# TensorE's order through attention, one norm chain for q and k, and a 16-byte offset in a hybrid decoder layer

## The chip, the cores and the metric

The kernel runs on one core of one Trainium2 chip. The metric is the device time of one execution in microseconds; three executions before the change took 2040.69, 2043.23 and 2045.04 us, a median of 2043.23 us. All work is in fp32; TensorE (PE) multiplies, ScalarE (ACT) and VectorE (DVE) split weights and do the element-wise work, GpSimd (POOL) helps with a few products and issues small DMAs, and SyncE (SP) issues the weight loads.

## The reference

One decoder layer on 256 tokens of width 2048. An SSD (Mamba-2) branch and an attention branch run from the same normed input, are merged by sigmoid gates, and a causal ConvFFN follows. What matters here is the attention branch (one block of 256 keys, so it is plain causal attention with a relative bias):

```python
q = rmsnorm(q, q_norm_w) * (D ** -0.5)          # 16 heads, D = 128
k = rmsnorm(k, k_norm_w)
s_own = jnp.einsum('bhqd,bhkd->bhqk', qi, kown)
s_own = jnp.where(dist >= 0, s_own + bias_own, -jnp.inf)
p = jax.nn.softmax(logits, axis=-1)
out = jnp.einsum('bhqk,bhkd->bhqd', p_own, vown)
...
y_attn = moba_attention(q, k, v, ...) @ w_attn_out[l]
x = x + (g_ssm * y_ssm + g_attn * y_attn) @ w_out[l]
```

## The kernel before

**Units.** Every weight matrix is streamed once, in units of 128 x 2048 floats (1 MB). For each unit SP loads `wraw`; for each of its two halves ACT writes a rounded high part `whi` (line 181) and DVE the rest, the low part `wlo` (line 182), both in the matmul's fp32r type, three buffers each. `cm_chunk` (lines 211 to 219) then multiplies a half: for each of 8 blocks of 128 columns the high part meets the high and the low part of the activations (lines 215 and 216), and 8 matmuls with the low part follow (line 218). A unit is 48 matmuls of 128x128 weights and 256 moving columns. `tm_chunk` (lines 371 to 383) does the same for the values v with 512 moving columns, 24 matmuls for a unit.

**Stages.** Three of four parts of v; eight head pairs (`attn_pair(j)`, four units each: q, q, k, k), with the last part of v between pairs 5 and 6; six units of the attention gate; sixteen units of `wao` with ten more gate units among them; the SSD branch in eight groups; `wso`, whose last quarter (q = 3) runs without other work in between; `wout`; the FFN's up and down parts.

**Attention's own work** is hung between units by `Spread`: a list of steps is added with a number of units, and `sp.tick()`, called after each unit, traces the next share of every list, in the order in which the lists were added. For a pair these are: the sums of squares (`sums`, line 451), the norm (`norm`, line 462: one small matmul with `sel`, line 466, then a chain of DVE and ACT operations, a transpose, a product by POOL for q and by DVE for k, line 479, and the split into `qhl` or `khl`, lines 481 and 482), the `scores` (10 matmuls for two heads, lines 500, 501 and 229 to 231), `soft`, the transposes of the probabilities (`ptr`, 6 PE operations, lines 529 to 531) and the product with the values (`pv`, 8 matmuls, lines 546 to 549). The norm of q stands one unit after q's last unit, the norm of k one unit after k's, the scores two units after that, `ptr` two later, `pv` one later. "A seam" below is a place at which such matmuls stand between those of the units.

**Order.** A planner puts the instructions of each engine in order, from the order of the text and its own costs. `tc.issue_after(last_mm[0].ins)` forbids it to place attention's matmuls ahead of the unit matmul traced before them, but lets it place them later, in the middle of a unit too. PE, ACT, DVE and POOL each run their queue in that order and wait at its head.

Of the kernel before, what the change touches and what calls it, by code (L numbers as in the profile page):

```python
# [124 lines left out]
class Spread:  # L125
# [2 lines left out]
    def __init__(self):  # L128
        self.work = []

    def add(self, gen, units):
        self.work.append([list_steps(gen), units])

    def tick(self):
        for w in self.work:
# [24 lines left out]
def _body(tc, nc, d, out):  # L160
# [7 lines left out]

    last_hi = [None]

    def unit(src, n=2048, before=None):
        raw = base.tile([128, 2048], F32, name="wraw", bufs=3)
        if before is None:
            nc.sync.dma_start(raw[:, :n], src)
        parts = []
        for c in range(2):
            hi = base.tile([128, 1024], F32R, name="whi", bufs=3)
            lo = base.tile([128, 1024], F32R, name="wlo", bufs=3)
            if before is None:
                s = slice(c * n // 2, (c + 1) * n // 2)  # L180
                last_hi[0] = S.activation(hi[:, :n // 2], raw[:, s], AF.Copy)  # L181
                V.tensor_tensor(lo[:, :n // 2], raw[:, s], hi[:, :n // 2].bitcast(F32), op=SUB)  # L182
            else:
                split_with_x(raw, src, hi, lo, c, before)
            parts.append((hi, lo))
        return parts
# [13 lines left out]
    def after_hi():  # L200
        return tc.issue_after(last_hi[0].ins) if last_hi[0] is not None else contextlib.nullcontext()

    last_mm = [None]

    def mm_tile():
        return psum.tile([128, 512], F32, name="mm", bufs=4)

# [3 lines left out]
    def cm_chunk(ps, part, xh, xl, k0, nk, first, last):  # L211
        hi, lo = part
        for k in range(nk):
            w = hi[:, k * 128:(k + 1) * 128]
            PE.matmul(ps, w, xh[:, k0 + k], start=first and k == 0, stop=False)  # L215
            PE.matmul(ps, w, xl[:, k0 + k], start=False, stop=False)  # L216
        for k in range(nk):
            last_mm[0] = PE.matmul(ps, lo[:, k * 128:(k + 1) * 128], xh[:, k0 + k], start=False,  # L218
                                   stop=last and k == nk - 1)

    def cm_unit(src, xh, xl, nk=16):
        parts = unit(src, nk * 128)
        ps = mm_tile()[:, :T]
        for c in range(2):
            cm_chunk(ps, parts[c], xh, xl, c * nk // 2, nk // 2, c == 0, c == 1)
        return ps
# [144 lines left out]
    def tm_chunk(pst, part, k0, first, last):  # L371
        hi, lo = part
        for k in range(2):
            wh = hi[:, k * 512:(k + 1) * 512]
            for tt in range(2):
                ts = slice(tt * 128, (tt + 1) * 128)
                PE.matmul(pst[tt], hph[:, k0 + k, ts], wh, start=first and k == 0, stop=False)  # L377
                PE.matmul(pst[tt], hpl[:, k0 + k, ts], wh, start=False, stop=False)  # L378
        for k in range(2):
            wl = lo[:, k * 512:(k + 1) * 512]  # L380
            for tt in range(2):
                ts = slice(tt * 128, (tt + 1) * 128)
                last_mm[0] = PE.matmul(pst[tt], hph[:, k0 + k, ts], wl, start=False, stop=last and k == 1)  # L383


    def tm_units(srcs, after_unit, before=None, mid=None):
# [54 lines left out]
    def attn_pair(j):  # L441
        st = {}
# [7 lines left out]

        def sums(key):
            def f():
                t = ap.tile([128, 16], F32, name="part", bufs=2)
                V.tensor_reduce(t, st["s" + key].rearrange("p h (b i) -> p (h b) i", i=32), axis=AX.X, op=ADD,
                                apply_transpose=True)
                t2 = ap.tile([128, 2, 16], F32R, name="part2", bufs=2)
                S.activation(t2[:, 0], t, AF.Copy)
                V.tensor_tensor(t2[:, 1], t, t2[:, 0].bitcast(F32), op=SUB)
                st["t" + key] = t2
            return f  # L460

        def norm(key):
            def f():
                ps = c_tile()
                with tc.issue_after(last_mm[0].ins):
                    PE.matmul(ps[:, 0:32], sel.rearrange("p a b -> p (a b)"),
                              st["t" + key].rearrange("p a b -> p (a b)"), start=True, stop=True)
                v = ap.tile([128, 2, 8], F32, name="nv", bufs=2)
                V.tensor_tensor(v, ps[:, 0:16].rearrange("p (h b) -> p h b", b=8),
                                xe[:, None, :].to_broadcast([128, 2, 8]), op=ADD)  # L470
                V.tensor_tensor(v, ps[:, 16:32].rearrange("p (h b) -> p h b", b=8), v, op=ADD)
                r = rsq(ap, v, [128, 2, 8], "nv", bufs=2)
                w = ap.tile([128, 2, T], F32, name="rw", bufs=2)
                V.transpose(w.rearrange("p h (b i) -> p (h b) i", i=32),
                            r.rearrange("p h b -> p (h b)")[:, :, None].to_broadcast([128, 16, 32]))
                n = st["n" + key]

                E = nc.gpsimd if key == "q" else V
                E.tensor_tensor(n, n, w, op=MUL)  # L479
                t = ap.tile([128, 2, 2, T], F32R, name=key + "hl", bufs=1)  # L480
                S.activation(t[:, 0], n, AF.Copy)
                E.tensor_tensor(t[:, 1], n, t[:, 0].bitcast(F32), op=SUB)
                st[key] = t
            return f

        def load_bias():
            st["b"] = ap.tile([128, 2, 256], F32, name="bias", bufs=1)
# [4 lines left out]
        def scores(h):  # L492
            def f():
                q, k = st["q"][:, :, h], st["k"][:, :, h]
                ps = c_tile()

                k2 = k[:, :, 0:128]
                po = ps[:, 0:256].rearrange("p (a t) -> p a t", t=128)
                with tc.issue_after(last_mm[0].ins):
                    PE.matmul(po, q[:, 0, 0:128], k2, start=True, stop=False)  # L500
                    PE.matmul(po, q[:, 1, 0:128], k2, start=False, stop=True)
                    mm3(ps[:, 256:512], q[:, 0, 128:], q[:, 1, 128:], k[:, 0], k[:, 1])
                p = ap.tile([128, 384], F32, name="p", bufs=2)
                mx = ap.tile([128, 2], F32, name="mx", bufs=2)
                V.tensor_tensor(p[:, 0:128], ps[:, 128:256], st["b"][:, h, 128:256], op=ADD)
                V.tensor_tensor_reduce(p[:, 0:128], ps[:, 0:128], p[:, 0:128], 1.0, -3.0e38, ADD, MAX, mx[:, 0:1])
                V.tensor_tensor_reduce(p[:, 128:384], ps[:, 256:512], st["b"][:, h], 1.0, -3.0e38, ADD, MAX,
                                       mx[:, 1:2])
                V.tensor_scalar(mx, mx, -1.0, None, op0=MUL)
                st["p", h], st["mx", h] = p, mx  # L510
            return f
# [12 lines left out]
        def ptr(h):  # L524
            def f():
                p = st["p", h]
                ps = c_tile()
                with tc.issue_after(last_mm[0].ins):
                    PE.transpose(ps[:, 0:128], p[:, 256:384], ident)
                    PE.transpose(ps[:, 128:256], p[:, 0:128], ident)  # L530
                    PE.transpose(ps[:, 256:384], p[:, 128:256], ident)
                t = pts[h]
                S.activation(t[:, 0], ps[:, 0:384], AF.Copy)
                V.tensor_tensor(t[:, 1], ps[:, 0:384], t[:, 0].bitcast(F32), op=SUB)
            return f

        def pv(h):
            def f():
# [3 lines left out]
                hc = slice((2 * j + h) * 128, (2 * j + h + 1) * 128)  # L542
                po = c_tile().rearrange("p (a t) -> p a t", t=T)

                with tc.issue_after(last_mm[0].ins):
                    PE.matmul(po, vh[:, 0, hc], t[:, :, 128:384], start=True, stop=False)
                    PE.matmul(po[:, :, 128:], vh[:, 1, hc], t[:, :, 0:128], start=False, stop=False)
                    PE.matmul(po[:, :, 128:], vl[:, 1, hc], t[:, :, 0:128], start=False, stop=False)
                    PE.matmul(po[:, 0], vl[:, 0, hc], t[:, 0, 128:384], start=False, stop=True)
                o = st["o"]  # L550
                S.activation(o[:, h], po[:, 1], AF.Copy)
                V.tensor_tensor(o[:, h], po[:, 0], o[:, h], op=ADD)
# [5 lines left out]
        for i in range(4):  # L558
            key = "qk"[i // 2]
            evac(key, i % 2, cm_unit(d["wqk"][j, i], hph, hpl))  # L560
            if i == 1:
                sp.add([[sums("q"), load_bias], norm("q")], 2)
            if i == 3:
                sp.add([sums("k"), norm("k"), [], [scores(0), scores(1), soft(0), soft(1)], [], [ptr(0), ptr(1)],
                        [pv(0), pv(1)]], 7)
            sp.tick()

    sp = Spread()
    tick = lambda u: sp.tick()
    for j in range(8):  # L570
        if j == 6:
            evac(3, tm_units(d["wv"][3], tick))
# [25 lines left out]
    for o in range(6):  # L598
        gl[o] = gate_attn(o)
        sp.tick()  # L600
    sp.flush()
    attn.close()

    hnt, hnh, hnl = r32("hn")
# [25 lines left out]
    for o in range(KT):  # L630
        if o >= 6:
            gl[o] = gate_attn(o)
            sp.tick()
        po = cm_unit(d["wao"][o], oh_, ol_)
        g = gl.pop(o)
        V.tensor_tensor(g, g, po, op=MUL)
        if o % 2:
# [206 lines left out]
        return steps  # L844

    def out_unit(q, u, done):
        parts = unit(d["wso"][q, u])
        yh, yl = yt[:, q % 2, 0], yt[:, q % 2, 1]
        ps = mm_tile()
        for c in range(2):  # L850
# [184 lines left out]
```

## Time and profile before

| | us |
|---|---|
| median of three executions | 2043.23 |
| the profiled execution, its own time | 2042.42 |
| the span of that execution | 2040.6 |
| PE busy | 2027.8 |
| DVE busy | 1499.0 |
| ACT busy | 1199.7 |
| POOL busy | 75.9 |

PE's matmuls overlap one another, so that a busy PE can still be slower or faster: the number of matmuls in a stretch of time tells more than the busy time. The granted clock of TensorE over the span is 0.999. Views used below: the page, the busy time by stretch, the waits, the chain of work that ended last in order of time, the groups of instructions and the timeline.

### The profile page before, as it was taken

How to read it: one execution, taken by the hardware profiler on the slowest of the kernel's cores; microseconds unless marked ns; L12 is line 12 of the kernel's file. 1: busy time of each engine (PE TensorE's matmuls, PEld its weight loads, DVE VectorE, ACT ScalarE, POOL GpSimd, SP SyncE). 2: the span in 40 equal slices, each digit the busy share in tenths (PEclk: the TensorE clock that was granted, in tenths of full speed). 3: DMA queues.
4: the chain of work that ended last, by engine and by line, in shares of the span. 5: the costliest groups of instructions: out<-in, count | busy, mean ns of one | idle time of the engine just before them, and what ended most of it. 6: DMA issues, size and time to landing. Idle time of an engine off the chain costs nothing.

```text
span 2040.6 us, 40859 instructions
## 1 busy us (share of the span) xinstructions
PE 2027.8 (99%) x17211; PEld 2002.9 (98%) x17211; DVE 1499.0 (73%) x2256; ACT 1199.7 (59%) x1669; POOL 75.9 (4%) x99
## 2 busy tenths in 40 slices
PE   9999999999999999999999999999999999999999
PEld 7998999999999999999999999999999999999999
DVE  7568877646697888888988987677777765677554
ACT  6456566544569677676676655565555553455333
POOL 0002111000000000000000000000000000000000
PEclk9999999999999999999999999999999999999999
DMA  7753455655555565565555585555555555555555
GB/s 282 256 189 140 174 177 187 236 200 190 198 198 205 203 209 203 181 212 192 194 205 192 181 280 192 198 195 188 200 192 190 203 186 196 197 189 200 191 181 170
DMA packets 65056, 405.55 MB, mean 199 GB/s; under 512 B 7671, under 2 KB 10280, under 8 KB 21352
## 3 DMA queue, kind: packets, MB, share of 16 engines
q1 hardware_dynamic: 55384, 376.56, 51.9%
q0 software_dynamic: 6464, 22.11, 3.5%
q10 hardware_dynamic: 3024, 4.27, 0.6%
q8 instruction: 134, 2.20, 0.4%
q14 instruction: 50, 0.41, 0.1%
HBM read 397.58 MB, written 8.48 MB: 199 GB/s over the span
## 4 chain that ended last, share of the span: by engine, by line
PE 95%; issue 3%; DVE 1%; ACT 1%; POOL 0%; DMA 0%; DVEq 0%; POOLq 0%
PE mm L215 29%; PE mm L218 29%; PE mm L216 29%; PE mm L383 1%; PE mm L377 1%; PE mm L378 1%; PE cc L804 1%; DVE wlo L182 0%; PE cc L805 0%; PE cc L757 0%; DMA xw<-x 0%; PE cc L231 0%; PE cc L230 0%; PE cc L229 0%; POOL nq L479 0%
## 5 line engine op out<-in xcount | busy, mean ns | idle before, releaser
L181 ACT ACTIVATE whi<-wraw 128x1024 fp32r<-128x1024 f32 (+1 forms) x712 | 745.9, 1050 | 694.0 <-PE mm L216 605.1
L182 DVE TENSOR_TENSOR wlo<-wraw,whi 128x1024 fp32r<-128x1024 f32 (+1 forms) x712 | 865.0, 1217 | 259.2 <-ACT whi L181 254.3
L215 PE MATMUL mm<-hn,whi 128*128 128x256 f32 x1536 | 360.1, 277 | 0.0
L216 PE MATMUL mm<-hn,whi 128*128 128x256 f32 x1536 | 359.8, 277 | 0.0
L216 PE MATMUL mm<-fh,whi 128*128 128x256 f32 x1408 | 327.8, 276 | 0.0
L215 PE MATMUL mm<-fh,whi 128*128 128x256 f32 x1408 | 327.8, 276 | 0.0
L215 PEld LDWEIGHTS mm<-hn,whi 128*128 128x128 f32 x1536 | 288.6, 188 | 1.6 <-ACT whi L181 0.2
L216 PEld LDWEIGHTS mm<-hn,whi 128*128 128x128 f32 x1536 | 288.6, 188 | 0.1
L216 PEld LDWEIGHTS mm<-fh,whi 128*128 128x128 f32 x1408 | 264.3, 188 | 0.0
L215 PEld LDWEIGHTS mm<-fh,whi 128*128 128x128 f32 x1408 | 264.3, 188 | 0.0
L218 PE MATMUL mm<-hn,wlo 128*128 128x256 f32 x1536 | 206.4, 277 | 0.0
L218 PEld LDWEIGHTS mm<-hn,wlo 128*128 128x128 f32 x1536 | 189.2, 188 | 0.0
L218 PE MATMUL mm<-fh,wlo 128*128 128x256 f32 x1408 | 188.2, 276 | 0.0
L215 PE MATMUL mm<-hp,whi 128*128 128x256 f32 x768 | 184.1, 281 | 0.0
L216 PE MATMUL mm<-hp,whi 128*128 128x256 f32 x768 | 183.1, 279 | 0.0
L218 PEld LDWEIGHTS mm<-fh,wlo 128*128 128x128 f32 x1408 | 172.7, 188 | 0.0
L215 PE MATMUL mm<-a,whi 128*128 128x256 f32 x704 | 164.3, 276 | 0.0
L216 PE MATMUL mm<-a,whi 128*128 128x256 f32 x704 | 164.3, 276 | 0.0
L216 PEld LDWEIGHTS mm<-hp,whi 128*128 128x128 f32 x768 | 145.1, 189 | 0.1
L215 PEld LDWEIGHTS mm<-hp,whi 128*128 128x128 f32 x768 | 145.1, 189 | 0.1
L215 PEld LDWEIGHTS mm<-a,whi 128*128 128x128 f32 x704 | 132.1, 188 | 0.0
L216 PEld LDWEIGHTS mm<-a,whi 128*128 128x128 f32 x704 | 132.1, 188 | 0.0
(307 smaller groups left out, 3271.9 us busy)
## 6 DMA issues: line engine op xcount, KB each, us to landing
wraw<-wup SPq DMA_DIRECT2D x88, 1024.0 KB, 4.8
wraw<-wssd SPq DMA_DIRECT2D x80, 1024.0 KB, 4.9
wraw<-wqk SPq DMA_DIRECT2D x32, 1024.0 KB, 4.8
wraw<-wso SPq DMA_DIRECT2D x32, 1024.0 KB, 5.0
wraw<-wd SPq DMA_DIRECT2D x32, 1024.0 KB, 4.8
wraw<-wga SPq DMA_DIRECT2D x16, 1024.0 KB, 4.9
wraw<-wao SPq DMA_DIRECT2D x16, 1024.0 KB, 5.1
wraw<-wgs SPq DMA_DIRECT2D x16, 1024.0 KB, 4.8
```

Of the source, the lines that this page charges most:

```text
L181: last_hi[0] = S.activation(hi[:, :n // 2], raw[:, s], AF.Copy)
L182: V.tensor_tensor(lo[:, :n // 2], raw[:, s], hi[:, :n // 2].bitcast(F32), op=SUB)
L215: PE.matmul(ps, w, xh[:, k0 + k], start=first and k == 0, stop=False)
L216: PE.matmul(ps, w, xl[:, k0 + k], start=False, stop=False)
L218: last_mm[0] = PE.matmul(ps, lo[:, k * 128:(k + 1) * 128], xh[:, k0 + k], start=False, stop=last and k == nk - 1)
L377: PE.matmul(pst[tt], hph[:, k0 + k, ts], wh, start=first and k == 0, stop=False)
L378: PE.matmul(pst[tt], hpl[:, k0 + k, ts], wh, start=False, stop=False)
L383: last_mm[0] = PE.matmul(pst[tt], hph[:, k0 + k, ts], wl, start=False, stop=last and k == 1)
L804: PE.matmul(ps, x0, m[:, :, h, 0:256], start=True, stop=False)
```

## The change

1. Through the eight pairs, the last part of v and the six gate units, PE's order is that of the text (`tc.manual_schedule` on TensorE alone); the `issue_after` blocks and `last_mm` go. The other engines' order is still planned.
2. q and k of a pair share one norm chain: one `part`, one split of it, one matmul with `sel` (64 columns in place of two times 32), one chain on 32 columns in place of two on 16. The products of k and q both go to POOL, k first; k's low part stays on DVE and q's on POOL.
3. The steps stand at two places: after the first unit of a pair (the norm of the pair before and `ptr` of the pair before that) and after its third (`pv`, then `scores`).
4. A `wlo` buffer grows from 1024 to 1056 columns (128 bytes more for each of three). In the first half of `wao`'s first unit, and of the first unit of `wso`'s last quarter, the low part starts 4 columns (16 bytes) into it.

```diff
-    def add(self, gen, units):
-        self.work.append([list_steps(gen), units])
+    def add(self, gen, units, first=False):
+        self.work.insert(0 if first else len(self.work), [list_steps(gen), units])
...
+    def unit(src, n=2048, before=None, shift=False):
...
-            lo = base.tile([128, 1024], F32R, name="wlo", bufs=3)
+            lo = base.tile([128, 1056], F32R, name="wlo", bufs=3)
+            o = 4 if shift and c == 0 else 0
+            lo = lo[:, o:o + 1024]
...
         def sums(key):
             def f():
+                if key == "q":
+                    st["p"] = ap.tile([128, 2, 16], F32, name="part", bufs=2)
+                V.tensor_reduce(st["p"][:, int(key == "k")], st["s" + key].rearrange("p h (b i) -> p (h b) i", i=32),
+                                axis=AX.X, op=ADD, apply_transpose=True)
             return f
+        def split_sums():
+            t2 = ap.tile([128, 2, 32], F32R, name="part2", bufs=2)
+            p = st["p"].rearrange("p a b -> p (a b)")
+            S.activation(t2[:, 0], p, AF.Copy)
+            V.tensor_tensor(t2[:, 1], p, t2[:, 0].bitcast(F32), op=SUB)
+            st["t"] = t2
+        def norm_sum():
+            st["ps"] = c_tile()
+            PE.matmul(st["ps"][:, 0:64], sel.rearrange("p a b -> p (a b)"),
+                      st["t"].rearrange("p a b -> p (a b)"), start=True, stop=True)
+        def norm():
...
+            r = rsq(ap, v, [128, 4, 8], "nv", bufs=2)
+            for i, key in enumerate("kq"):
                 w = ap.tile([128, 2, T], F32, name="rw", bufs=2)
+                h = 2 - 2 * i
                 V.transpose(w.rearrange("p h (b i) -> p (h b) i", i=32),
+                            r[:, h:h + 2].rearrange("p h b -> p (h b)")[:, :, None].to_broadcast([128, 16, 32]))
                 n = st["n" + key]
+                nc.gpsimd.tensor_tensor(n, n, w, op=MUL)
+        def split():
+            for key in "kq":
+                n = st["n" + key]
                 t = ap.tile([128, 2, 2, T], F32R, name=key + "hl", bufs=1)
                 S.activation(t[:, 0], n, AF.Copy)
+                E = V if key == "k" else nc.gpsimd
                 E.tensor_tensor(t[:, 1], n, t[:, 0].bitcast(F32), op=SUB)
                 st[key] = t
...
             if i == 1:
-                sp.add([[sums("q"), load_bias], norm("q")], 2)
+                sp.add([[sums("q"), load_bias]], 1)
             if i == 3:
-                sp.add([sums("k"), norm("k"), [], [scores(0), scores(1), soft(0), soft(1)], [], [ptr(0), ptr(1)],
-                        [pv(0), pv(1)]], 7)
+                sp.add([[sums("k"), split_sums], [norm_sum, norm], split], 3, first=True)
+                sp.add([[], [], [], [scores(0), scores(1), soft(0), soft(1)], [], [ptr(0), ptr(1)], [],
+                        [pv(0), pv(1)]], 8)
...
+    order = contextlib.ExitStack()
+    order.enter_context(tc.manual_schedule(engines={nc.tensor.engine}))
     for j in range(8):
...
     sp.flush()
+    order.close()
...
-        po = cm_unit(d["wao"][o], oh_, ol_)
+        po = cm_unit(d["wao"][o], oh_, ol_, shift=o == 0)
...
-        parts = unit(d["wso"][q, u])
+        parts = unit(d["wso"][q, u], shift=q == 3 and u == 0)
```

More of the change, by code (lines that the diff above doesn't have):

```diff
@@ L169, in _body @@
     last_hi = [None]
-    def unit(src, n=2048, before=None):
+    def unit(src, n=2048, before=None, shift=False):
         raw = base.tile([128, 2048], F32, name="wraw", bufs=3)
@@ L201, in after_hi @@
         return tc.issue_after(last_hi[0].ins) if last_hi[0] is not None else contextlib.nullcontext()
-    last_mm = [None]
     def mm_tile():
@@ L217, in cm_chunk, with cm_unit @@
         for k in range(nk):
[L218 to L222, printed above, removed]
+            PE.matmul(ps, lo[:, k * 128:(k + 1) * 128], xh[:, k0 + k], start=False, stop=last and k == nk - 1)
+    def cm_unit(src, xh, xl, nk=16, shift=False):
+        parts = unit(src, nk * 128, shift=shift)
         ps = mm_tile()[:, :T]
@@ L382, in tm_chunk @@
                 ts = slice(tt * 128, (tt + 1) * 128)
-                last_mm[0] = PE.matmul(pst[tt], hph[:, k0 + k, ts], wl, start=False, stop=last and k == 1)
+                PE.matmul(pst[tt], hph[:, k0 + k, ts], wl, start=False, stop=last and k == 1)
     def tm_units(srcs, after_unit, before=None, mid=None):
@@ L452, in f @@
             def f():
[L453 to L459, printed above, removed]
-            return f
@@ L462, in norm @@
[L462 to L472, printed above, removed]
+                if key == "q":
+                    st["p"] = ap.tile([128, 2, 16], F32, name="part", bufs=2)
@@ new lines, in norm_sum @@
+        def norm_sum():
[3 more added lines that the diff above has]
+        def norm():
+            ps = st["ps"]
+            v = ap.tile([128, 4, 8], F32, name="nv", bufs=2)
+            V.tensor_tensor(v, ps[:, 0:32].rearrange("p (h b) -> p h b", b=8),
+                            xe[:, None, :].to_broadcast([128, 4, 8]), op=ADD)
+            V.tensor_tensor(v, ps[:, 32:64].rearrange("p (h b) -> p h b", b=8), v, op=ADD)
+            r = rsq(ap, v, [128, 4, 8], "nv", bufs=2)
+            for i, key in enumerate("kq"):
@@ L473, in f @@
                 w = ap.tile([128, 2, T], F32, name="rw", bufs=2)
+                h = 2 - 2 * i
                 V.transpose(w.rearrange("p h (b i) -> p (h b) i", i=32),
-                            r.rearrange("p h b -> p (h b)")[:, :, None].to_broadcast([128, 16, 32]))
+                            r[:, h:h + 2].rearrange("p h b -> p (h b)")[:, :, None].to_broadcast([128, 16, 32]))
                 n = st["n" + key]
-                E = nc.gpsimd if key == "q" else V
-                E.tensor_tensor(n, n, w, op=MUL)
+                nc.gpsimd.tensor_tensor(n, n, w, op=MUL)
@@ L480, in f @@
+        def split():
+            for key in "kq":
+                n = st["n" + key]
                 t = ap.tile([128, 2, 2, T], F32R, name=key + "hl", bufs=1)
                 S.activation(t[:, 0], n, AF.Copy)
+                E = V if key == "k" else nc.gpsimd
                 E.tensor_tensor(t[:, 1], n, t[:, 0].bitcast(F32), op=SUB)
                 st[key] = t
-            return f
         def load_bias():
@@ L498, in f @@
                 po = ps[:, 0:256].rearrange("p (a t) -> p a t", t=128)
[L499 to L502, printed above, removed]
+                PE.matmul(po, q[:, 0, 0:128], k2, start=True, stop=False)
+                PE.matmul(po, q[:, 1, 0:128], k2, start=False, stop=True)
+                mm3(ps[:, 256:512], q[:, 0, 128:], q[:, 1, 128:], k[:, 0], k[:, 1])
                 p = ap.tile([128, 384], F32, name="p", bufs=2)
@@ L527, in f @@
                 ps = c_tile()
[L528 to L531, printed above, removed]
+                PE.transpose(ps[:, 0:128], p[:, 256:384], ident)
+                PE.transpose(ps[:, 128:256], p[:, 0:128], ident)
+                PE.transpose(ps[:, 256:384], p[:, 128:256], ident)
                 t = pts[h]
@@ L543, in f @@
                 po = c_tile().rearrange("p (a t) -> p a t", t=T)
[L545 to L549, printed above, removed]
+                PE.matmul(po, vh[:, 0, hc], t[:, :, 128:384], start=True, stop=False)
+                PE.matmul(po[:, :, 128:], vh[:, 1, hc], t[:, :, 0:128], start=False, stop=False)
+                PE.matmul(po[:, :, 128:], vl[:, 1, hc], t[:, :, 0:128], start=False, stop=False)
+                PE.matmul(po[:, 0], vl[:, 0, hc], t[:, 0, 128:384], start=False, stop=True)
                 o = st["o"]
```

## The prediction

> **What bounds the kernel now.** I read the page first, for the share of PE, then the busy time by stretch, the waits of PE, and last the chain of work that ended last, in order of time.
>
> ```profile
> PE 2027.8 (99%) x17211; PEld 2002.9 (98%) x17211; DVE 1499.0 (73%) x2256; ACT 1199.7 (59%) x1669; POOL 75.9 (4%) x99
> ```
>
> PE is busy for 2027.8 of 2040.6 us, so time can only come from the few stretches in which PE stands, or from matmuls that run at a worse pace. The busy time by stretch has both. Its columns are start and end, length, then busy time and number of instructions for each engine, the granted clock and the DMA share.
>
> ```profile
> 73.20:343.60 270.40, 262.73 (x2132) 255.89 (x2131) 199.96 (x413) 167.59 (x331) 39.59 (x31) 0.99 0.50 178
> 139.00:161.00 22.00, 18.09 (x148) 17.14 (x146) 18.00 (x44) 15.07 (x36) 6.81 (x5) 1.00 0.45 156
> 161.00:183.00 22.00, 19.79 (x152) 19.53 (x153) 19.11 (x60) 12.76 (x37) 5.14 (x5) 0.92 0.30 108
> 315.00:343.60 28.60, 27.75 (x237) 27.38 (x237) 21.20 (x43) 21.48 (x35) 1.29 (x1) 1.00 0.46 156
> 343.60:556.60 213.00, 213.00 (x1811) 213.00 (x1810) 128.77 (x166) 99.45 (x110) 9.54 (x16) 1.00 0.59 208
> 1324.50:2037.00 712.50, 712.50 (x6288) 712.46 (x6287) 476.10 (x672) 366.75 (x450) 0.00 (x0) 1.00 0.55 192
> ```
>
> The first row is attention with the six gate units, which end at 343.6: PE stands for 270.40 - 262.73 = 7.7 us in it. Of these 3.9 lie between 139 and 161, 2.2 between 161 and 183, 0.85 at the end. The clock in the third row is 0.92, which takes another 0.08 x 22 = 1.8 us. The fifth row, `wao` with its gates up to the SSD branch, has no idle time at all, but 213.00 / 1811 = 117.6 ns for a matmul; the last row, the FFN, has 712.50 / 6288 = 113.3 ns for matmuls of the same shape at the same clock. That is **4.3 ns each, 7.8 us over the stage**, and no busy time shows it.
>
> The waits of PE (engine and line, whom it waited for, us in total, times, longest) say who is late in attention:
>
> ```profile
> PE cc L500 <- DVE khl L482: 5.8, 3, 2.9
> PE cc L501 <- POOL qhl L482: 1.1, 1, 1.1
> PE cc L466 <- DVE part L458: 0.7, 3, 0.3
> ```
>
> Together they are 7.6 of the 7.7 us. The chain (start, us, what) shows the two paces and where one turns into the other: 8 low-part matmuls take 0.91 us or 0.94.
>
> ```profile
> 147.14 0.94 PE mm L218 x8
> ...
> 215.95 0.94 PE mm L218 x8
> 216.89 0.23 PE cc L546
> ...
> 219.89 0.91 PE mm L218 x8
> ...
> 266.89 0.91 PE mm L218 x8
> 267.80 0.24 PE cc L546
> ...
> 270.88 0.94 PE mm L218 x8
> ...
> 308.78 0.94 PE mm L218 x8
> ...
> 341.69 0.91 PE mm L218 x8
> ...
> 345.67 0.94 PE mm L218 x8
> ...
> 707.28 0.94 PE mm L218 x8
> 708.23 0.23 PE cc L288
> ...
> 710.28 0.91 PE mm L218 x8
> ```
>
> The pace holds over unit after unit, and turns at seams. A `pv` (L546) turned slow to fast at 216.9 and fast to slow at 267.8; the one after 341.69 left the slow pace on which all of `wao` runs. From 147.14 to 308.78 the chain lists 22 low-part rows of 0.94 or 0.96, each for a half unit of 24 matmuls: 22 x 24 x 4.3 ns = 2.3 us in attention.
>
> **The change part by part.** The sum is made against the profiled execution, 2042.42 us; the median of the runs is 2043.23, 0.8 more, and the same difference is taken off it.
>
> *Order and places.* The rows below are timelines (start, us, engine, line, what, in brackets the idle time before).
>
> ```profile
> 93.96 2.11 POOL L479 TENSOR_TENSOR nq<-nq,rw 128x512 f32<-128x512 f32 x1 [31.64 <-DVE rw L474]
> 142.44 0.61 ACT L481 ACTIVATE qhl<-nq 128x512 fp32r<-128x512 f32 x1
> 161.14 0.39 PE L500 MATMUL cc<-khl,qhl 128*128 128x256 f32 x1 [2.86 <-DVE khl L482]
> 210.88 0.25 PE L466 MATMUL cc<-part,sel 128*128 128x32 f32 x1 [0.20 <-DVE part L458]
> 218.56 0.68 DVE L482 TENSOR_TENSOR khl<-nk,khl 128x512 fp32r<-128x512 f32 x1
> 223.35 0.28 PE L500 MATMUL cc<-khl,qhl 128*128 128x256 f32 x1
> 324.15 0.36 PE L500 MATMUL cc<-khl,qhl 128*128 128x256 f32 x1 [0.85 <-DVE khl L482]
> 207.39 2.16 DVE L182 TENSOR_TENSOR wlo<-wraw,whi 128x1024 fp32r<-128x1024 f32 x1 [0.30 <-ACT whi L181]
> ```
>
> Pair 0's product of q was done at 96.07, but its split stands in ACT's queue at 142.44: the plan was 46 us late, pair 0's scores came only behind it, and pairs 1 and 2 followed too closely for their chains. Hence the stops at 161.14 and before. With PE's order as written the pairs stand four units apart, so **these stops go: -7.7 us, and the clock's -1.8** that followed the longest of them (2.86 us; the others drew none). I count the whole of both as gone and put new waits in separately.
>
> *New waits.* PE now waits at the head of its queue, and behind the waiting scores stand the next unit's matmuls, which free `whi`, `wlo` and `wraw`, so ACT, DVE and SP's loads stop as well after three buffers. Prices from the groups (count, busy, mean ns):
>
> ```profile
> L448 ACT ACTIVATE sq<-mm 128x256 f32<-128x256 f32 x32 | 11.7, 365 | 0.0
> L449 ACT ACTIVATE nk<-mm,kscale 128x256 f32<-128x256 f32 x16 | 7.5, 467 | 0.0
> L466 PE MATMUL cc<-part,sel 128*128 128x32 f32 x16 | 3.4, 213 | 0.7 <-DVE part L458 0.7
> L479 DVE TENSOR_TENSOR nk<-nk,rw 128x512 f32<-128x512 f32 x8 | 6.3, 791 | 0.2
> L479 POOL TENSOR_TENSOR nq<-nq,rw 128x512 f32<-128x512 f32 x8 | 12.0, 1502 | 66.7 <-DVE rw L474 47.6 <-PE mm L218 5.7 <-PE mm L383 5.7
> L482 POOL TENSOR_TENSOR qhl<-nq,qhl 128x512 fp32r<-128x512 f32 x8 | 11.6, 1451 | 51.6 <-ACT qhl L481 51.6
> ```
>
> Pair 0: if the plan is as late as now, ACT splits k and q only after the evacuation of the unit in front: 0.37 + 0.47 + 2 x 0.61, then POOL 1.45, 3.5 us; if it places them when their inputs are there, nothing. Before, this pair's scores waited 1.1 us for the same POOL operation. I take 2.3, between 1.1 and 3.5. The others have two units, `ptr` and `pv` between norm and scores, as at 210.88 and 223.35: 12.5 us. There k's chain took 218.56 + 0.68 - 210.88 = 8.4. Now k's product is POOL's (1.50 for 0.79, +0.7), q's follows it (+1.5) and q's split and POOL's low part end about 11.5: just in time. Pair 6 has no `ptr` and `pv` at its seams, some 10.9 us: 0.5 late. Pair 7 waits 0.85 even now; its chain grows by the same 3.1 (8.4 to 11.5) and gains 0.6 of room, as `ptr` now stands behind the norm, so between 0.85 and 3.3; I take 2.0, as half of the growth is POOL's, which does little else there. **Sum +4.8 us**; the ends are 0 and 2.3 for each of the eight, 18.4.
>
> *One chain.* Eight `sel` matmuls fewer. In the stream each is worth its pace rather than its 213 ns, so between 0 and 8 x 0.21 = 1.7 us; I take **-0.5**. Five small DVE and two ACT operations a pair go too, beside PE. K's product on POOL can hold up a weight split: the 2.16 us of 207.39 stand where DVE took 1.23 before, while POOL multiplied. Eight more such delays of 0.9 are 7 us of DVE, hidden, since DVE is busy for 200.0 of attention's 270.4 us; without that cover they would be PE's. The bias load keeps its place in POOL's queue, and none of SP's loads moves.
>
> *Pace in attention.* Seams become 18 where they are some 34, and most hold `pv` followed by `scores`, a pair that the trace never shows together. Ends: all fast, -2.3; all 38 units slow, 38 x 48 x 4.3 ns = 7.8, so +5.5. I take 0, nearest to the mixed pace of now.
>
> *The offset in `wao`.* The last seam still ends in a `pv` of fast units, so by 267.80 and 341.69 the slow pace would begin here. No row shows a weight load 16 bytes off. What the rows do show is that a short disturbance (one 0.23 us matmul, L288, at 708.23) is enough to turn slow to fast. So the ends are 0 and -7.8, with +1.0 below that should the eight moved loads themselves be slow (8 x 0.12). I take **-7.8**, as the only turns of a slow stream without other cause are by disturbances like it.
>
> Here the Trainium skill speaks against the change. SBUF — State Buffer, section Specifications, gives SBUF lines of 16 bytes, with a penalty for each crossing. By that rule an offset of one line crosses as many lines as none, the loads take what they took, and this term is 0 instead of -7.8.
>
> *The offset in `wso`.* It stands 25 units before the seam at 1324.5, at about 1188, where the pace is fast already. I take 0; if it turns fast to slow, 25 x 48 x 4.3 ns = 5.2 us up to that seam. The larger `wlo` moves all that is allocated behind it by up to 384 bytes; I take 0, as a multiple of 128.
>
> **Sum:** -7.7 - 1.8 + 4.8 - 0.5 + 0 - 7.8 = -13.0. From 2042.42 that is 2029.4, from the median **2030.2 us**.
>
> **The rivals.**
>
> *All of it works:* no new wait (+4.8 goes) and fast in attention too (-2.3): -20.1, 2023.1 us. For it: the chain fits into 12.5 us by the rows of pair 3. Against: pair 7 waits even with today's shorter chain.
>
> *The offset does nothing,* `wao` stays slow: -5.2, 2038.0 us. For it: the slow pace held through 213 us and some 37 changes of unit. Against: the turn at 708. This is also the case in which the change doesn't do what it says, and what the line rule of SBUF — State Buffer would give.
>
> *Every pair waits as pair 0 does:* +18.4 for +4.8, so +0.6 net, 2043.8 us, no change. For it: an order that PE can't leave, and a chain that ends within 1 us of its limit. Against: POOL is the only engine added, at 39.59 of 270.4 us.
>
> *Slower:* the offset in `wso` throws the fast stream into the slow pace and the seam at 1324.5 doesn't turn it back. Then 5.2 us and 6288 x 4.3 ns = 27.0 come on top: -13.0 + 32.2 = +19.2, 2062.4 us. It decides at that seam, an L288 like the one at 708.23, which did turn slow to fast; if it does so again only the 5.2 stay, 2035.4 us. The same price would be due if the moved addresses made the FFN slow.
>
> **How the numbers follow.** Forecast 0.38; all works 0.27; the offset does nothing 0.17; `wso` slow up to 1324.5 0.05; every pair waits 0.08; slow to the end 0.05. A difference of 0.2%, 4.1 us, is about what a measurement tells from no change. The first four are faster by more (the third by 0.26%, so I leave 0.02 of it within): **faster 0.85, same 0.10, slower 0.05**. The range takes in the first four with the bounds of the small terms: 2019 (all works, the whole 1.7 of the `sel` matmuls and two us of settling at fewer seams) to 2040; 13% lie above.
>
> **What would show it.** The stretch of attention about 6 us shorter, with no idle before the scores of pairs 1 to 5, a wait for `qhl` at pair 0 and at pair 7, and a clock of 1.00; low-part rows of 0.91 behind `wao`'s first unit; 0.91 through `wso`, `wout` and the FFN. Wrong would be: waits for `qhl` at every pair, 0.94 in `wao` or after 1188, or a pace in the SSD branch that differs from now.

## The result, and the profile after

The changed kernel is **slower**: a median of 2067.36 us (2065.83 to 2068.65, four runs) against 2042.84 us for the kernel before (2040.69 to 2045.04, four runs), a ratio of 1.012 with a 95% interval of 1.0102 to 1.0137. The forecast was 2030.2, with 2040 as the upper end of its range. The profiled execution of the changed kernel took 2068.65 us, 26.2 more than that of the kernel before, at a granted clock of 0.998 against 0.999.

The page's row of busy time for the changed kernel:

```profile
PE 2057.4 (100%) x17203; PEld 2034.0 (98%) x17203; DVE 1497.9 (72%) x2200; ACT 1197.0 (58%) x1645; POOL 89.4 (4%) x107
```

PE has eight instructions fewer (the `sel` matmuls), stands for 9.4 us of the span of 2066.8 in place of 12.8, and is nevertheless busy for 29.6 us more. The matmuls themselves have become slower. The busy time by stretch says where; first the changed kernel (start and end, length, busy time and count of PE, PEld, DVE, ACT and POOL, clock, DMA share and GB/s; the stretches are attention with its gates, `wao` with gates, the SSD branch up to its last seam, the end of `wso`, which is the eleven units from that seam to `wout`, then `wout`, and a part of the FFN):

```profile
75.40:338.40 263.00, 258.45 (x2122) 252.85 (x2121) 196.61 (x357) 163.98 (x307) 53.19 (x39) 0.99 0.52 183
338.40:479.90 141.50, 141.50 (x1250) 141.50 (x1250) 81.66 (x100) 66.66 (x72) 7.31 (x12) 1.00 0.61 217
479.90:1166.50 686.60, 686.60 (x5899) 683.56 (x5898) 580.07 (x847) 472.61 (x647) 22.13 (x41) 1.00 0.57 197
1166.50:1229.00 62.50, 62.50 (x532) 62.46 (x531) 50.57 (x64) 33.21 (x39) 4.84 (x9) 1.00 0.75 257
1229.00:1319.40 90.40, 90.40 (x769) 90.40 (x769) 57.22 (x80) 46.82 (x64) 0.00 (x0) 1.00 0.54 187
1326.00:2038.50 712.50, 712.50 (x6064) 712.50 (x6063) 465.03 (x656) 357.02 (x438) 0.00 (x0) 1.00 0.54 188
```

The same stretches of the kernel before, as far as they were not shown:

```profile
343.60:490.60 147.00, 147.00 (x1250) 147.00 (x1249) 81.63 (x100) 66.66 (x73) 7.32 (x12) 1.00 0.60 210
490.60:1171.90 681.30, 681.27 (x5899) 677.73 (x5898) 579.33 (x847) 472.10 (x647) 22.19 (x41) 1.00 0.57 198
1171.90:1232.00 60.10, 60.10 (x532) 60.06 (x531) 50.55 (x64) 33.09 (x39) 4.85 (x9) 1.00 0.76 267
1232.00:1319.00 87.00, 87.00 (x770) 87.00 (x769) 57.20 (x80) 46.85 (x64) 0.00 (x0) 1.00 0.55 195
```

Attention and `wao` did become faster, by 6.8 and 5.5 us, and then all is lost again behind them, in stages whose code the change hardly touches. In 712.5 us of the FFN the kernel before did 6288 matmuls and this one 6064: 117.5 ns each for 113.3, with PE never idle and the clock at 1.00. Stage lengths, taken from the start of the first matmul of each in the two traces (for the end of `wso`, from that of the last seam of the SSD branch), add up to the whole difference:

| stage | before, us | after, us | difference |
|---|---|---|---|
| values v | 72.8 | 74.4 | +1.6 |
| attention and its gates | 269.8 | 262.9 | -6.8 |
| `wao` and gates | 147.0 | 141.5 | -5.5 |
| SSD branch | 681.3 | 686.7 | +5.3 |
| end of `wso` | 60.1 | 62.4 | +2.3 |
| `wout` | 87.0 | 90.5 | +3.4 |
| FFN | 718.2 | 744.0 | +25.8 |
| sum | | | +26.1 |

(The 1.6 us of v aren't the change's: over the fourteen kernels of this study that stage took 72.7 to 74.6 us, whatever was in them.)

The waits of PE in the changed kernel:

```profile
PE cc L509 <- DVE khl L493: 2.2, 1, 2.2
PE cc L510 <- POOL qhl L493: 1.6, 2, 1.0
PE cc L509 <- ACT qhl L491: 0.7, 1, 0.7
```

The scores (now L509 and L510) wait for 4.5 us in all, at two pairs only, where PE stood for 7.7 us before. The chain of the work that ended last, in order of time, has the pace (in the changed kernel the unit matmuls are L216, L217 and L219, `pv` begins at L553, the SSD's product is L817 and L818):

```profile
330.11 0.91 PE mm L219 x8
...
333.56 0.94 PE mm L219 x8
...
337.33 0.23 PE cc L553
...
343.13 0.91 PE mm L219 x8
...
1147.83 0.91 PE mm L219 x8
1148.74 0.23 PE cc L817
...
1151.31 0.94 PE mm L219 x8
...
1155.08 0.23 PE cc L817
...
1157.63 0.91 PE mm L219 x8
...
1165.79 0.91 PE mm L219 x8
1166.69 0.23 PE cc L288
1168.81 0.94 PE mm L219 x8
...
1324.28 0.94 PE mm L219 x8
1325.22 0.23 PE cc L288
...
1327.34 0.94 PE mm L219 x8
```

The last `pv` turned the slow stream fast, and `wao` ran fast. In the SSD branch the seams of L817 turn it slow and fast by turns; in the kernel before the same seams (L804 there) left it fast. The seam at 1166.69 (L288, on the tile `nsp`) turns it slow, and that of 1325.22 (L288 again, on `ssp`) leaves it slow. It stays so until 2002, where the pace turns without a seam. The two offset halves did not begin this: that of `wso` comes at 1185.6, 19 us behind the turn.

### The profile page after: what moved, and what is told of

Read it like the earlier page. It is cut to its first block, busy times and chain, and to the rows that moved or that the text cites. A ratio compares the mean times of both kernels' runs of the same rounds, so it can differ in the third digit from the quotient of the medians.

```text
span 2066.8 us, 40766 instructions
## 1 busy us (share of the span) xinstructions
PE 2057.4 (100%) x17203; PEld 2034.0 (98%) x17203; DVE 1497.9 (72%) x2200; ACT 1197.0 (58%) x1645; POOL 89.4 (4%) x107
## 4 chain that ended last, share of the span: by engine, by line
PE 99%; issue 0%; POOL 0%; DMA 0%; ACT 0%; DVE 0%; DVEq 0%; POOLq 0%
PE mm L216 30%; PE mm L217 30%; PE mm L219 30%; PE mm L377 1%; PE mm L378 1%; PE mm L383 1%; PE cc L817 1%; PE cc L818 0%; PE cc L770 0%; DMA xw<-x 0%; PE cc L230 0%; PE cc L229 0%; PE cc L231 0%; PE cc L553 0%; PE cc L510 0%
## 5 line engine op out<-in xcount | busy, mean ns | idle before, releaser
L216 PE MATMUL mm<-hn,whi 128*128 128x256 f32 x1536 | 363.2, 278 | 0.0
L217 PE MATMUL mm<-hn,whi 128*128 128x256 f32 x1536 | 362.9, 278 | 0.0
L216 PE MATMUL mm<-fh,whi 128*128 128x256 f32 x1408 | 339.7, 281 | 0.0
L217 PE MATMUL mm<-fh,whi 128*128 128x256 f32 x1408 | 339.4, 281 | 0.0
L216 PEld LDWEIGHTS mm<-hn,whi 128*128 128x128 f32 x1536 | 289.3, 188 | 1.1
L217 PEld LDWEIGHTS mm<-hn,whi 128*128 128x128 f32 x1536 | 289.3, 188 | 0.1
L217 PEld LDWEIGHTS mm<-fh,whi 128*128 128x128 f32 x1408 | 266.5, 189 | 0.0
L216 PEld LDWEIGHTS mm<-fh,whi 128*128 128x128 f32 x1408 | 266.4, 189 | 0.0
L219 PE MATMUL mm<-hn,wlo 128*128 128x256 f32 x1536 | 208.1, 278 | 0.0
L219 PE MATMUL mm<-fh,wlo 128*128 128x256 f32 x1408 | 194.5, 280 | 0.0
L219 PEld LDWEIGHTS mm<-hn,wlo 128*128 128x128 f32 x1536 | 190.7, 188 | 0.0
L216 PE MATMUL mm<-hp,whi 128*128 128x256 f32 x768 | 181.7, 279 | 0.0
L217 PE MATMUL mm<-hp,whi 128*128 128x256 f32 x768 | 180.9, 278 | 0.0
L219 PEld LDWEIGHTS mm<-fh,wlo 128*128 128x128 f32 x1408 | 178.0, 188 | 0.0
L216 PE MATMUL mm<-a,whi 128*128 128x256 f32 x704 | 168.7, 280 | 0.0
L217 PE MATMUL mm<-a,whi 128*128 128x256 f32 x704 | 168.6, 280 | 0.0
L216 PEld LDWEIGHTS mm<-hp,whi 128*128 128x128 f32 x768 | 145.4, 189 | 0.1
L217 PEld LDWEIGHTS mm<-hp,whi 128*128 128x128 f32 x768 | 145.4, 189 | 0.1
L217 PEld LDWEIGHTS mm<-a,whi 128*128 128x128 f32 x704 | 133.0, 189 | 0.0
L216 PEld LDWEIGHTS mm<-a,whi 128*128 128x128 f32 x704 | 132.9, 189 | 0.0
```

## The experiments

The theory, once this trace was read: **what turns the pace at a seam is the place in SBUF of what the seam's matmuls read.** The larger `wlo` moves all that is allocated behind it by 3 x 128 = 384 bytes in each partition; `pt`, `mhl`, `nsp` and `ssp`, the moving operands of L553, L817 and L288, lie there. The prediction had taken that for a multiple of 128 and so for nothing. The rivals: the offset of 16 bytes, `wlo`'s own new places, and PE's new order. A stream of 6336 matmuls in the FFN at 4.3 ns more each is 27 us, so that a single execution tells most of these apart.

Each kernel ran beside the kernel before on the same chip (2046.18 us for the first four, 2042.52 for the next four, a median of 2043.89 from ten runs for the last four). f2 and f4 were timed in several executions, the other kernels once; the ten runs of the kernel before lie between 2042.23 and 2045.72 us, so a single time is good to some 3 us. Stage lengths behind attention agree far better between traces, to about 0.3 us.

### Part by part

**e1_layout_only** is the kernel before with the larger buffers alone:

```diff
-            lo = base.tile([128, 1024], F32R, name="wlo", bufs=3)
+            lo = base.tile([128, 1056], F32R, name="wlo", bufs=3)[:, :1024]
```

> The kernel before with one edit: the wlo buffers have 1056 columns (their places move by 0, 128 and 256 bytes, all pools behind them by 384); no offset, no new order. If the places in memory make the loss: the attention stage as before, then seams of the SSD branch that leave the slow pace and a slow FFN, some +30 us over before (about 2073). If the new order makes it: within 4 us of before.

2075.35 us against 2046.18: a loss of 29.2 us with neither the new order nor an offset. The SSD branch took 686.65 us, the end of `wso` 62.42, `wout` 90.45 and the FFN 743.96, the numbers of the changed kernel to the second digit; `wao` was fast here too (141.46). Attention stayed at 271.3. So the whole loss is the layout's, and the gain in attention is the order's.

**e2_after_1024** is the changed kernel with `wlo` back at 1024 columns, hence without the offset:

```diff
-            lo = base.tile([128, 1056], F32R, name="wlo", bufs=3)
-            o = 4 if shift and c == 0 else 0
+            lo = base.tile([128, 1024], F32R, name="wlo", bufs=3)
+            o = 0
```

> The kernel after with wlo buffers of 1024 columns and no offset, so the new order and the one norm chain alone, at the old places. If places make the loss: all seams of the SSD branch and the FFN fast as before, attention and wao as after (about 5 us and 8 us shorter than before), so about 2030. If the new order makes it: as after, 2067.

2036.30 us, 9.9 below the kernel before. The SSD branch and all behind it are as before (FFN 718.21), attention keeps its gain (263.8), and `wao` is slow again (146.99).

**e3_after_no_offset** keeps the larger buffers and drops the offset:

```diff
-            o = 4 if shift and c == 0 else 0
+            o = 0
```

> The kernel after with buffers of 1056 columns and no offset anywhere. If the offsets do nothing (in after the stream is fast when it comes to the one in wao, and stays slow behind the one in wso): as after, within 3 us of 2067. If the offset in wao is what keeps wao fast: +8, 2075. If the offset in wso is what makes the FFN slow: 2035.

2066.20 us, with every stage behind attention within 0.1 us of the changed kernel, `wao` too (141.46). The offset neither caused the loss nor, in this layout, brought the fast `wao`: the stream came fast out of the last `pv`, whose operand had moved. The fourteen traces bear this out: with `pt` moved by 384 bytes (the changed kernel, e1, e3, e5, e6, e7, f2) the stream left the last `pv` fast in all seven, whether it came slow (four of them) or fast (three); in the other seven it came fast and left slow.

**e4_after_pad128** keeps all of the change and adds a tile of 128 bytes in front of the pools, so that the tiles of the pools behind it are moved by 512 bytes in place of 384:

```diff
+    base.tile([128, 32], F32, name="pad9")
```

> The kernel after with 128 bytes of padding behind the wlo buffers, so that everything behind them moves by 512 bytes in place of 384 and only the wlo buffers themselves stand elsewhere within 512 bytes. If the places of the other tiles within 512 bytes decide: SSD branch and FFN fast, about 2035. If the places of the wlo buffers decide: as after, about 2067.

2027.77 us, 18.4 below the kernel before and some 40 below the changed kernel, for 128 bytes that nothing reads. The SSD branch took 678.5 us, the FFN 718.21. At the end of attention the stream turned slow, and this time the offset had something to do; the chain in e4 (in e4, f1 and f4 the lines behind the pad are one higher than in the changed kernel):

```profile
335.08 0.91 PE mm L219 x8
335.99 0.23 PE cc L554
...
339.07 0.95 PE mm L219 x8
...
341.84 0.91 PE mm L219 x8
```

The eight matmuls of 339.07 are those of the offset half. Before them stand sixteen at 0.12, behind them all of `wao` at 0.91.

### Is it the place, and modulo what

Two kernels move the pools of the kernel before by a pad alone; `wlo` stays where it was.

**e5_pools_384:**

```diff
+    base.tile([128, 96], F32, name="pad9")
```

> The kernel before with 384 bytes of padding behind the wlo buffers: wlo stands where it stood, all pools behind it move as in after. If the pools' places decide: as the run with the wider wlo buffers alone, wao fast, about 2120 slow matmuls in the SSD branch, slow wso, wout and FFN, about 2075. If it takes the moved wlo buffers too: as before, 2045.

**e8_pools_256:**

```diff
+    base.tile([128, 64], F32, name="pad9")
```

> The kernel before with 256 bytes of padding behind the wlo buffers. If a place counts within 256 bytes: every stage as before, within 3 us of it. If it counts within 512 bytes: other seams turn, and SSD branch or FFN differ from before by more than 5 us.

Moved by 384 bytes, 2074.37 us (against 2042.52): SSD 686.5, `wout` 90.45, FFN 746.4, slow to its end. Moved by 256 bytes, 2043.71: SSD 681.1, `wout` 87.04, FFN 718.21, the kernel before. So `wlo`'s own places are not needed for the loss. A move of 256 or 512 bytes (e8, e4) changes nothing in these stages, one of 384 does: what counts is the place within 256 bytes, as far as steps of 128 can tell. The larger `wlo` shows only at the end: the turn at 2002, which the changed kernel, e1, e3, e6 and e7 have, is missing in e5, 2.4 us, and in g1 below. Whether `wlo`'s own place makes that turn, or that of something next to it, no run separates.

Then single operands, in the changed kernel.

**e6_nsp_moved** moves `nsp`, and `ab` and `mhl`, which are allocated behind it, by another 128 bytes:

```diff
-            st["sq"] = sum_split(sd, sqt[:, 0], "nsp", tag="cb")
+            t = sd.tile([128, 2 * T + 32], F32R, name="nsp", tag="cb")[:, 32:].rearrange("p (a t) -> p a t", t=T)
+            S.activation(t[:, 0], sqt[:, 0], AF.Copy)
+            V.tensor_tensor(t[:, 1], sqt[:, 0], t[:, 0].bitcast(F32), op=SUB)
+            st["sq"] = t
```

> The kernel after with the moving operand of the SSD norm's matmul (nsp) 128 bytes further, where it stands 512 bytes from its old place; ab and mhl behind it move by 128 bytes too, all else stays. If the operand of the last seam sets the pace of what follows: wso's last quarter and wout fast (8 us less), the FFN slow again from its own seam, whose operand stands as in after, so about 2057. If the pace comes from elsewhere: as after, 2067.

2053.79 us, and the busy time by stretch of e6 (SSD; the end of `wso` with `wout`; FFN) shows the loss cut in two:

```profile
479.20:1157.60 678.40, 678.34 (x5900) 675.01 (x5900) 579.25 (x847) 472.00 (x647) 22.13 (x41) 1.00 0.56 199
1157.60:1304.70 147.10, 147.10 (x1299) 147.06 (x1298) 107.78 (x144) 79.88 (x102) 4.84 (x9) 1.00 0.63 224
1312.00:2024.50 712.50, 712.50 (x6064) 712.50 (x6064) 464.13 (x656) 356.96 (x439) 0.00 (x0) 1.00 0.53 187
```

147.1 us for the end of `wso` and `wout` is the 60.1 + 87.0 of the kernel before, and the SSD branch is fast throughout. The FFN has 6064 matmuls in 712.5 us again: its own seam turned the fast stream slow.

**e7_ssp_moved** moves `ssp`, and with it the tiles allocated behind it, which PE does not read:

```diff
+    fp.tile([128, 32], F32, name="pad9")
```

> The kernel after with the moving operand of the FFN norm's matmul (ssp) 128 bytes further, 512 from its old place, and nothing else that TensorE reads moved. If that operand sets the pace of the FFN: wso and wout slow as in after, the FFN fast from its seam on (25.8 us less), about 2041. If the FFN keeps the pace it gets from wout: as after, 2067.

2067.59 us, no change: the FFN was to be fast and stayed slow. The stream came slow from `wout`, and the seam on `ssp`, now at its old place within 256 bytes, left it as it came:

```profile
1323.22 0.94 PE mm L219 x8
1324.16 0.23 PE cc L288
...
1326.28 0.94 PE mm L219 x8
```

I had supposed that this seam makes the stream fast whatever arrives. It does not; at its old place it only kept a fast one fast.

**f2_nsp_ssp_moved** has both edits, all of the change; it was timed in several executions:

> The kernel after with both norm operands (nsp and ssp) 128 bytes further, 512 from their old places, wlo and its offsets as in after. If these operands carry the whole loss: SSD branch, wso, wout and FFN fast, about 2028, 15 us under the kernel before. If each seam only passes on what comes, or the wider wlo costs something by itself: wout or the FFN slow, over 2040.

A median of 2029.56 us (2026.69 to 2031.74), a ratio of 0.9933 with an interval of 0.9917 to 0.995: **the loss is gone, and the change is a gain of 0.7%.** Its busy time by stretch (attention, `wao`, SSD, FFN):

```profile
74.10:336.20 262.10, 257.51 (x2122) 252.01 (x2121) 196.65 (x357) 163.77 (x307) 53.19 (x39) 0.99 0.52 183
336.20:477.70 141.50, 141.50 (x1250) 141.50 (x1249) 81.69 (x100) 66.67 (x72) 7.30 (x12) 1.00 0.61 217
477.70:1156.00 678.30, 678.24 (x5899) 674.91 (x5898) 579.33 (x847) 471.83 (x647) 22.13 (x41) 1.00 0.57 199
1310.00:2022.50 712.50, 711.68 (x6280) 711.48 (x6278) 475.82 (x674) 365.45 (x448) 0.00 (x0) 1.00 0.54 192
```

**g1_before_ssp** is the other direction: the kernel before, with `ssp` moved by 128 bytes, by the pad of e7.

> The kernel before with the operand of one matmul (ssp, line 288 of the FFN norm) 128 bytes further and no other operand of TensorE moved. If the place of that one operand sets the pace of the whole FFN: every stage up to wout as before, the FFN slow, +26 us, about 2069. If it takes more than one operand: as before, 2043.

2073.36 us against 2043.89: one operand of one matmul among 17211 costs some 29 us. The chain of g1 at that seam, and its FFN in the busy time by stretch:

```profile
1326.75 0.91 PE mm L218 x8
1327.65 0.23 PE cc L288
...
1329.77 0.94 PE mm L218 x8
...
1332.59 0.94 PE mm L218 x8
```

```profile
1328.00:2040.50 712.50, 712.50 (x6051) 712.50 (x6051) 464.48 (x655) 356.50 (x439) 0.00 (x0) 1.00 0.53 187
```

The seam takes the same 0.23 us as ever, and the FFN behind it (746.1 us) has the slow pace to its end. All stages ahead of it, from `wao` on, are those of the kernel before. The tiles behind `ssp` moved too, and VectorE and ScalarE use most of them in the FFN's up part; they did not make the turn, since the first of them to be written, `fr`, is written only about 2 us after the slow pace had begun at 1327.88:

```profile
1329.85 0.42 ACT L305 ACTIVATE fr<-ssum 128x256 f32<-128x256 f32 x1 [0.24 <-DVE ssum L956]
```

Counted seam by seam, the fourteen traces agree. With `nsp` at +384 bytes (the changed kernel, e1, e3, e5, e7) all 40 of its seams turned a fast stream slow; in the other nine kernels 70 of 72 met a fast stream and left it fast. With `mhl` at +384 (the same five) each of the 160 seams of L817 turned the pace, 80 fast to slow and 80 slow to fast; the other 288 were met fast and left fast. `ssp` at +128 or +384 turned a fast stream slow both times that it met one (g1, e6); at 0, +256 or +512 it left a fast one fast all seven times.

### The offset by itself, and the wait that is left

**f1_pad128_no_offset** is e4 without the offset:

```diff
-            o = 4 if shift and c == 0 else 0
+            o = 0
```

> The kernel after with the 128 bytes of padding (all pools back within 256 bytes) and without the two offsets. In the padded kernel the last pv left the slow pace and the stream turned fast right behind the 8 low parts that stand 16 bytes off. If those turned it: wao slow, about 1247 slow matmuls, +8 us over the padded kernel with offsets. If the places of the wlo buffers did: wao fast all the same.

2036.70 us, 8.9 above e4. The chain of f1 at the place shown for e4:

```profile
335.36 0.91 PE mm L219 x8
336.27 0.24 PE cc L554
...
339.34 0.94 PE mm L219 x8
...
342.17 0.94 PE mm L219 x8
```

The same turn to slow, and nothing that ends it: `wao` took 146.99 us for 141.57 (5.4) and the SSD branch, which it entered slow, 681.8 for 678.5 (3.3). In a fast stream the offset costs next to nothing: 14 matmuls at the slow pace in the `wso` of e4, 0.07 us in the stage (60.15 for 60.08).

**f4_pair0_dve** is e4 with POOL's three operations of pair 0, two products and q's low part, on DVE, against the longest wait that is left, that of pair 0's scores:

```diff
-                nc.gpsimd.tensor_tensor(n, n, w, op=MUL)
+                (V if j == 0 else nc.gpsimd).tensor_tensor(n, n, w, op=MUL)
...
-                E = V if key == "k" else nc.gpsimd
+                E = V if key == "k" or j == 0 else nc.gpsimd
```

> The padded kernel with pair 0's products and q's low part on DVE in place of POOL. If PE waits at pair 0 because the plan holds POOL busy there: the wait of about 3.5 us before pair 0's scores and the half clock behind it go, 3 to 5 us less than the padded kernel, about 2024. If the chain itself is late: the wait stays and the time too, 2028.

A median of 2038.67 us, 0.9971 of the kernel before (0.996 to 0.9982) and some 11 us above e4. The scores of pair 0 did start without a wait, but a longer one took its place; waits of PE in f4, then two timelines, of POOL and of DVE:

```profile
PE cc L538 <- issue: 11.5, 1, 11.5
```

```profile
128.62 1.26 POOL L486 TENSOR_TENSOR nk<-nk,rw 128x512 f32<-128x512 f32 x1 [65.97 <-DVE rw L483]
129.83 0.77 POOL L501 DMA_DIRECT2D bias<-brep  x1
```

```profile
132.95 0.49 DVE L515 TENSOR_TENSOR p<-cc,bias 128x128 f32<-128x128 f32 x2 [0.49 <-DMA bias<-brep]
```

`ptr` (L538) of pair 0 needs the softmax, which needs the bias, and POOL's queue has the load of that bias behind its first product. That product is now pair 1's: POOL idles for 66 us, multiplies at 128.62, and only then issues the load. In the changed kernel the same load stood behind pair 0's product and was issued at 107.97. The order of POOL, which is still planned, is what is late, and moving work away from it moved the lateness to a load that PE's fixed order cannot go around.

## Why the prediction was wrong

**The step that failed** is one term: "The larger `wlo` moves all that is allocated behind it by up to 384 bytes; I take 0, as a multiple of 128." The mechanism that the prediction had read from the trace (two paces that hold over units and turn at seams) was right; this term of its sum was mis-sized. It measures +38.8 us in the medians: the changed kernel stands 24.5 above the kernel before (2067.36 against 2042.84), f2 with the same edits, and `nsp`, `mhl` and `ssp` put back within 256 bytes, 14.3 below it (2029.56 against 2043.89). The whole move, with `wao`'s gain from `pt` in it, is 34.4: e2, with the new order at the old places, is 9.9 below its kernel before. e1 and e5 give it without the rest of the change (+29.2 and +31.9, after a gain of 5.5 in `wao`), g1 gives its largest part by one tile. That a multiple of 128 costs nothing was not read from any run; 128 and 384 bytes cost, 256 and 512 did not. No row of the profile of before could show which place is a good one. But the rows had shown that a pace once turned holds for hundreds of microseconds, and `ssp`, one of the tiles that moved, is read at the very seam that stands before the FFN. The term deserved both ends, as the offset's had: 6288 x 4.3 ns = 27 us for the FFN alone.

**The slower rival** came out at almost this time (2062.4 us), with 5.2 us for the 5.7 measured in the end of `wso` and `wout` and 27.0 for the FFN's 25.8, and its last sentence named the moved addresses. Its cause was wrong, so that the agreement is in part luck: it put the turn on `wso`'s offset, which comes after the turn. It got 0.05 because the seam before the FFN was expected to make a slow stream fast again, as the seam at 708.23 had done; e7 shows that seam at its old place leaving a slow stream slow.

**Order and places** came as forecast and a little better: attention is 6.8 us shorter (f2: 7.7; e4: 8.0) where the terms gave -5.2. The stops at 161.14 and before are gone, none of pairs 1 to 6 waits, and those that I put in are there. Pair 0 waits 2.2 us for `khl` and 0.6 for `qhl` (forecast 2.3), pair 7 0.7 and 1.0 (forecast 2.0), pair 6 not at all (forecast 0.5): 4.5 us for 4.8.

**The clock** was not saved. I let 1.8 us go with the longest stop; the new waits draw it again. A stretch around pair 0's scores in the changed kernel:

```profile
108.00:132.00 24.00, 21.16 (x160) 20.73 (x159) 14.94 (x29) 11.68 (x24) 4.25 (x5) 0.86 0.48 156
```

0.14 x 24 = 3.4 us. In f2, with the same waits, pair 0's scores drew nothing, and those of pair 7 half as much; that stretch of f2:

```profile
310.00:334.00 24.00, 22.31 (x176) 21.81 (x176) 18.06 (x35) 17.83 (x29) 5.88 (x4) 0.93 0.46 172
```

0.07 x 24 = 1.7 us. Eight traces have nearly these waits, one execution each (the changed kernel, e2, e3, e4, e6, e7, f1, f2). The clock over 24 us at pair 0's scores was 1.00 in four of them, 0.93 in two and 0.86 in two, so some 2 to 3 us of this kind look like chance; what decides it no run shows.

**Pace in attention** was taken as 0; 687 slow matmuls (528 by the prediction's rows) became 191, which is 496 x 4.3 ns = 2.1 us gained. With idle time (7.7 to 4.5, -3.2) and the clock (+1.6) that explains 3.7 of the 6.8 us; the eight `sel` matmuls (0.5 forecast) and 13 seams fewer (33 became 20) are in the other 3.1, which no run separates.

**The offset in `wao`** does what was forecast where the stream arrives slow: 8.7 us between e4 and f1 in `wao` (5.4) and the SSD branch (3.3), for the 7.8 forecast. The prediction called the 213 us of that forecast `wao`, but `wao` ends at 490.61, and the rest up to 556.6 is the start of the SSD branch, which the slow pace also covered. The Trainium skill (SBUF — State Buffer, section Specifications) gives lines of 16 bytes and a penalty for each crossing. The conclusion drawn from that page, that a shift by one line changes nothing, is not borne out: the stream turned behind the eight shifted loads in e4 and did not in f1, and in a fast stream their eight matmuls took 0.95 us (the changed kernel) for 0.91 (e3). In the changed kernel the 5.5 us of `wao` came from the moved `pt` instead (e3), and the offset did nothing there. In `wso` it was forecast at 0 and cost 0.07 us in e4; in the changed kernel it met a slow stream and did not free it.

**The rest of the sum** was -13.0 us. f2, timed four times, stands at -14.3, but in part by luck: its `wao` is fast by the moved `pt` and not by the offset. e4, where the offset does what was forecast, ran once and stands at -18.4 against one run of the kernel before; its stages give -8.0 in attention for -5.2, and -8.2 in `wao` and the SSD branch for -7.8. "All of it works" (-20.1) did not come true, as pairs 0 and 7 wait in both.

**What stays open:** why the place of an operand within 256 bytes turns the pace, and which places do it in general. The `pv` of the earlier pairs show no rule as simple as that of the last one: at the old place some turned the stream slow (267.80 in the kernel before) and some fast (216.89). Only steps of 128 bytes and one offset of 16 were tried, and a place that is good for one arriving pace need not be so for the other.

## What to carry to other kernels

When a buffer changes its size, compare the addresses of all that lies behind it, and keep what moves at the same place modulo 256 bytes, which was enough here, or time a few pads of 128 bytes before judging an edit: here 128 bytes in front of two tiles decided between 1.2% slower (the changed kernel) and 0.7% faster (f2) for the same work. Read busy time together with the number of matmuls in each stage, since a pace that is 4% worse shows as no wait, no idle time and no lower clock. When one engine's order is fixed by hand, look at the loads that the other engines' queues still hold behind work; a wait removed at one step may only uncover such a load at the next.

## What the runs showed of the hardware

- The stream of 128x128 weights and 256 moving columns has two stable paces at the full clock, 113.3 and 117.5 ns a matmul. It held either over more than 6000 matmuls, and one matmul of 0.23 us decided which (g1).
- That matmul's effect depends on its moving operand's place: at +128 bytes the FFN lost 28 us (718.2 to 746.1), at +256 and +512 (e8, e4, where all was moved) nothing.
- The effect depends on the arriving pace too: `ssp` at its old place within 256 bytes kept a fast stream fast (f2) and a slow one slow (e7), and the 160 seams of L817 with `mhl` at +384 turned a fast stream slow and a slow one fast. The last `pv` goes by its place: with `pt` at +384 it left the stream fast from either pace, in seven kernels of seven.
- Eight weight loads 16 bytes off turned a slow stream to fast in `wao` (e4 against f1, 8.7 us in the stages) and did not turn the one in the changed kernel's `wso`.
- The same stop of 2.2 us was followed by a lower clock in one execution (0.86 over 24 us) and by none in another (f2).
